# Joining the block inverses: which transposes VectorE runs first

## The chip, the cores and the metric

The kernel runs on one core of one Trainium2 chip. The metric is the device time of one execution in microseconds. The time before is the median of three runs, 4732.12 us (4730.72 to 4736.02).

## The reference, cut to what matters

The reference is a two-layer encoder trunk over two sequences of 1024 tokens (width 1024). Each layer projects its normalised input once, gives the columns to four mixers (A attention, B RWKV-7, C Mamba-2, D gated delta rule), gates their outputs and projects back. B and D run in both directions of time. D solves a unit triangular system in each chunk of 64 tokens:

```python
kb = k * beta[..., None]
m = jnp.where(strict, jnp.einsum('bhcld,bhcsd->bhcls', kb, k) * decay, 0.0)
tmat = m + jnp.eye(L, dtype=f32)
rhs = jnp.concatenate([v * beta[..., None], kb * jnp.exp(gc)[..., None]], axis=-1)
sol = lax.linalg.triangular_solve(tmat, rhs, left_side=True, lower=True)
```

B is a token-by-token scan in the reference (`S = S * w + (S a) b + v k`, output `S r`). The kernel computes it in chunks of 64 tokens too, with the same kind of triangular system.

## The kernel before, in words

**Inverses.** Each direction of B and of D needs the inverses of 64 unit triangular 64x64 matrices (4 heads, 16 chunks). The matrices lie as two halves `h` of 64 partitions with 32 matrices (`y`) each. `invert` (L529) gathers the two 32x32 diagonal blocks of each matrix with four VectorE transposes (L536) and inverts all blocks at once with 31 steps of two VectorE operations (L543, L544); the result is `r`, with 32 partitions for each of the four pairs of half and block. `merge` (L546), which this text calls the joining, makes the 64x64 inverses from them. Four transposes, one for each 32 partitions, put the inverted diagonal blocks back into `dst` (L551). Two more, one for each half, make the transposed copy `Tr` of one of the two blocks, shown in the profile as `mT` (L556). Then, for two groups `g` of 16 matrices: 32 first products on TensorE for each half (L565, off-diagonal block of the source times `Tr`) into a PSUM bank; a ScalarE copy for each half to `Qs`, shown as `mQ` (L567); 32 second products for each half (L571, `Qs` times the other diagonal block, read from `dst`); and a VectorE copy for each half of the result into the off-diagonal place of `dst` (L573). All products are 32x32x32. The PSUM pool has three banks (tag `b`), `mQ` and `mT` have one buffer each.

For D the source is `SC` and `dst` lies in `GT`, which the profile writes as `GT<-SC`; before the joining, GpSimd clears the opposite corner of `dst` (L1137) and VectorE writes the masked products beside it in `GT` (L1138, two operations). For B source and `dst` are the same tile `G`, and `r` is `iR`. What follows the joining is the chain over the 16 chunks (`gdn_chain`, `rwkv_chain`), whose first step reads the joined inverses.

**Units and sides.** There are four units, two sequences in each of two layers. In a unit the mixers form two serial strings that run beside each other: D then A on one side, C then B on the other (`mixers`, L590). Each unit has two joinings in D and two in B, so the program has 16.

**Background.** The projections into the mixers and out of them (`in_tile`, `out_tiles`) are L472 matmuls into `pj`. They belong to the next or the last unit and are laid beside the mixers (`ahead`, `behind`, `mix`, from L1646). `paced` (L470) binds them in groups of 5 or 8: the first matmul of a group releases a GpSimd memset of a token (L476), and the next group but one waits for it. Weights of the projections are split into two parts by ScalarE (L342) and VectorE (L343), and finished tiles are copied out by ScalarE (L325, L328) and VectorE (L326).

**Order of the work.** Nothing is ordered by hand within an engine. The program is written once, each instruction takes a priority from its place in the text, and a planner with a simulated timeline (`schedule_with_timeline_sim`, L1735) places the instructions of each engine in one fixed order when the kernel is built: of those that are ready in its timeline, the one with the first priority. Dependencies by the data are kept. `urgent()` (L484) moves a part ahead of all others; `invert`, `merge` and the chains after them are urgent, and so are the copies out of `pj` and the splitting of weights. All DMAs are issued from the SP queue (L145); the joining issues none.

Of the kernel before, what the change touches and what calls it, by code (L numbers as in the profile page):

```python
# [106 lines left out]
class Body:  # L107
# [438 lines left out]
    def merge(self, pool, psp, r, d, src, dst):  # L546

        nc = self.nc
        for q in range(4):
            h, j = q // 2, q % 2  # L550
            nc.vector.transpose(dst[h][32 * j:32 * j + 32, :, 32 * j:32 * j + 32].rearrange("p y t -> p t y"), r[32 * q:32 * q + 32].rearrange("p j t -> p t j"))  # L551
        a, b = (0, 32) if d == 0 else (32, 0)
        Tr = self.t(pool, [128, 32, 32], tag="mT")
        for h in range(2):
            A = slice(64 * h + a, 64 * h + a + 32)
            nc.vector.transpose(Tr[A].rearrange("p y j -> p j y"), r[A])  # L556
        for g in range(2):
            gs = slice(g * 16, g * 16 + 16)
            Qs = self.t(pool, [128, 16, 32], tag="mQ")
            p1 = [self.t(psp, [128, 512], tag="b") for _ in range(2)]  # L560
            at = [(64 * h + a, 64 * h + b) for h in range(2)]
            AB = [(slice(pa, pa + 32), slice(pb, pb + 32)) for pa, pb in at]
            for i in range(16):
                for h, (A, B) in enumerate(AB):
                    nc.tensor.matmul(p1[h][B, i * 32:i * 32 + 32], src[h][a:a + 32, g * 16 + i, b:b + 32], Tr[A, g * 16 + i, :], start=True, stop=True, tile_position=at[h])  # L565
            for h, (A, B) in enumerate(AB):
                nc.scalar.copy(Qs[B].rearrange("p i t -> p (i t)"), p1[h][B])  # L567
            p2 = [self.t(psp, [128, 512], tag="b") for _ in range(2)]
            for i in range(16):
                for h, (A, B) in enumerate(AB):  # L570
                    nc.tensor.matmul(p2[h][A, i * 32:i * 32 + 32], Qs[B, i, :], dst[h][b:b + 32, g * 16 + i, b:b + 32], start=True, stop=True, tile_position=at[h][::-1])  # L571
            for h, (A, B) in enumerate(AB):
                nc.vector.tensor_copy(dst[h][a:a + 32, gs, b:b + 32], p2[h][A].rearrange("p (i t) -> p i t", t=32))  # L573
# [1168 lines left out]
```

## Time and profile before

| | |
|---|---|
| median of 3 runs | 4732.12 us |
| profiled execution | 4724.56 us |
| its span | 4722.7 us |
| mean granted TensorE clock | 0.892 of full |
| busy: PE, weight load, VectorE, ScalarE, GpSimd | 89%, 67%, 64%, 38%, 8% |
| transposes of L551 | 64, 144.5 us |
| DMA traffic | 192 GB/s over the span |

The span is the stretch from the first to the last recorded instruction of the profiled execution, and the time of that execution holds 1.9 us around it. PE is TensorE, PEld its weight loads, which lie beside the matmuls. In rows in order of time, `x32` is a number of equal instructions merged into one row, and a bracket gives the idle time of the engine before the row and what ended it. The clock is that which the chip granted to TensorE, 1.0 being 2.4 GHz and 0.5 being 1.2 GHz.

### The profile page before, as it was taken

Reading aid. Unit: us, or ns where it says so; the run is one execution under the profiler, and the core shown is the slowest. Engines: PE = TensorE matmul, PEld = TensorE weight load, DVE = VectorE, ACT = ScalarE, POOL = GpSimd, SP = SyncE. Lnnn points to the kernel's source line nnn. Section 1 sums busy time; section 2 is a strip of 40 time slices with the busy share of each in tenths; the row PEclk is TensorE's granted clock in tenths of the full one; section 3 lists DMA queues with packets and bytes.
Section 4 is the critical chain, followed back from the end, with each engine's and each line's share of the span. In section 5 each row is a group of like instructions: output and inputs, shape, how many; then the busy total and the mean of one; then the engine's idle time right before and its main releaser. Section 6 shows DMA issues by size and latency. Waiting matters only on the chain. (4 is left out here: it accounts for less than half of the span.)

```text
span 4722.7 us, 98675 instructions
## 1 busy us (share of the span) xinstructions
PE 4204.5 (89%) x38484; PEld 3184.7 (67%) x38484; DVE 3013.8 (64%) x6237; ACT 1817.7 (38%) x4054; POOL 381.8 (8%) x2073
## 2 busy tenths in 40 slices
PE   6889988999998997989989898989897989979897
PEld 3667666667676776745757666867675766767676
DVE  2369487466479587477438858656743876865765
ACT  2432434462431434443434242435333324434433
POOL 0111001000011000000011100000001110000001
PEclk8899976998998987989989898889798999979898
DMA  5787764552676666564657665566355757665635
GB/s 211 283 257 250 244 180 147 182 151 72 196 233 209 201 206 191 176 194 148 225 193 243 243 220 159 182 189 189 106 179 180 233 202 228 205 210 159 175 112 171
DMA packets 518089, 912.85 MB, mean 193 GB/s; under 512 B 152312, under 2 KB 268536, under 8 KB 514040
## 3 DMA queue, kind: packets, MB, share of 16 engines
q1 hardware_dynamic: 517624, 906.54, 59.9%
q8 instruction: 305, 5.00, 0.4%
q14 instruction: 160, 1.31, 0.1%
HBM read 622.85 MB, written 283.43 MB: 192 GB/s over the span
## 5 line engine op out<-in xcount | busy, mean ns | idle before, releaser
L472 PE MATMUL pj<-hh,w 128*128 128x512 f32 (+1 forms) x4096 | 1431.1, 420 | 61.0 <-POOL token L476 27.6
L472 PEld LDWEIGHTS pj<-hh,w 128*128 128x128 f32 (+1 forms) x4096 | 785.0, 195 | 268.1 <-issue 40.8
L472 PE MATMUL pj<-hl,w 128*128 128x512 f32 (+1 forms) x2048 | 856.4, 418 | 16.5 <-POOL token L476 16.2
L472 PEld LDWEIGHTS pj<-hl,w 128*128 128x128 f32 (+1 forms) x2048 | 399.7, 195 | 116.3 <-POOL token L476 25.2
L476 POOL MEMSET token<- 1x1 f32 x1613 | 143.7, 89 | 3244.3 <-PE pj L472 3235.6
L472 PE MATMUL pj<-w,hh 128*128 128x256 f32 x1536 | 334.5, 308 | 9.3 <-POOL token L476 6.0
L472 PEld LDWEIGHTS pj<-w,hh 128*128 128x128 f32 x1536 | 261.6, 204 | 32.2 <-issue 9.4
L472 PE MATMUL pj<-w,hl 128*128 128x256 f32 x960 | 267.0, 305 | 0.2 <-DVE hl L377 0.2
L328 ACT COPY st<-pj 128x512 f32<-128x512 f32 (+1 forms) x192 | 111.6, 581 | 328.6 <-PE pj L472 285.9
L1575 ACT ACTIVATE pT<-b 128x512 f32<-128x512 f32 x256 | 149.8, 598 | 222.9 <-PE b L1573 218.8
L652 DVE SCALAR_TENSOR_TENSOR cva<-cvi,cw,cva 128x1024 f32<-128x1024 f32 x144 | 183.7, 1280 | 69.1 <-ACT cva L648 44.7
L1541 DVE TENSOR_REDUCE mx<-b 128x1 f32<-128x512 f32 x256 | 169.2, 685 | 63.9 <-PE b L1540 62.3
L342 ACT CAST w<-w 128x512 fp32r<-128x512 f32 x160 | 98.9, 620 | 247.6 <-DMA w<-w_in 173.8
L472 PEld LDWEIGHTS pj<-w,hl 128*128 128x128 f32 x960 | 185.2, 203 | 11.6 <-issue 3.6
L343 DVE TENSOR_TENSOR w<-w,w 128x512 fp32r<-128x512 f32 x160 | 113.5, 710 | 121.2 <-ACT w L342 118.2
L1219 ACT ACTIVATE SE<-SC,el 64x64 f32<-64x64 f32 x480 | 141.1, 338 | 117.9 <-DVE SC L1230 59.7
L938 DVE TENSOR_TENSOR ZS<-us,SE 64x128 f32<-64x128 f32 x240 | 69.1, 288 | 160.8 <-PE us L931 142.1
L843 DVE SCALAR_TENSOR_TENSOR G<-b,Dk,mk 128x128 f32<-128x128 f32 x512 | 142.1, 343 | 37.1 <-PE b L838 36.5
L838 PE MATMUL b<-AR,BK 64*64 64x128 f32 x2048 | 158.4, 318 | 5.3 <-DVE G L843 5.1
L1584 PEld LDWEIGHTS b<-VO,pT 128*64 128x64 f32 x4096 | 138.1, 143 | 31.8 <-issue 25.4
L1584 PE MATMUL b<-VO,pT 128*64 128x65 f32 x4096 | 153.8, 230 | 0.4 <-DVE mx L1541 0.3
L838 PEld LDWEIGHTS b<-AR,BK 64*64 64x64 f32 x2048 | 115.3, 155 | 46.7 <-issue 37.4
(395 smaller groups left out, 8179.1 us busy)
## 6 DMA issues: line engine op xcount, KB each, us to landing
w<-win SPq DMA_DIRECT2D x384, 512.0 KB
win<-w SPq DMA_DIRECT2D x128, 512.0 KB
P<-st SPq DMA_DIRECT2D x248, 256.0 KB
w<-wout SPq DMA_DIRECT2D x96, 512.0 KB
w<-w_in SPq DMA_DIRECT2D x128, 256.0 KB
G<-P SPq DMA_DIRECT2D x112, 256.5 KB
x<-x SPq DMA_DIRECT2D x56, 512.0 KB
cvi<-P SPq DMA_DIRECT2D x48, 512.0 KB
```

What stands on the lines that cost most here:

```text
L328: nc.scalar.copy(st[0:M], ps[0:M])
L342: nc.scalar.copy(w2[:, 0], w)
L343: nc.vector.tensor_tensor(w2[:, 1], w, wf[:, 0], SUB)
L472: m = self.nc.tensor.matmul(*mm[:3], **mm[3]).ins
L476: t = self.nc.gpsimd.memset(self.token, 0.0).ins
L652: nc.vector.scalar_tensor_tensor(a, c[:, j:j + 1024], wt(j, i), a, MUL, ADD)
L838: nc.tensor.matmul(pss[x][self.half(x ^ a), i * 128:i * 128 + 128], BK[self.half(x), pr, c, a], AR[self.half(x), pr, c].rearrange("p a t - ...
L843: v.scalar_tensor_tensor(G[:, x, pr, c, :], pss[x][:, i * 128:i * 128 + 128], Dk[:, c, 2 * x + pr:2 * x + pr + 1], mk, MUL, MUL)
L1219: nc.scalar.activation(SE[half(x), pr], VS[half(x), x, pr, i, :], AF.Identity, scale=el[half(x), d, pr, c:c + 1])
L1541: v.tensor_reduce(mx[:, n, qt:qt + 1], ps, AX.X, ALU.max, negate=True)
L1575: nc.scalar.activation(pT[kt], ps, AF.Exp)
L1584: nc.tensor.matmul(po[64 * x:64 * x + 64, i, :], pT[kt][:, o:o + 64], VO[:, kt, h, :], start=(kt == 0 and i == 0), stop=(kt == 7), skip_gr ...
```

## The change

In `merge` the loop of the four transposes into `dst` moves below the loop of the two transposes into `Tr`. Nothing else is changed.

```diff
     def merge(self, pool, psp, r, d, src, dst):
 
         nc = self.nc
-        for q in range(4):
-            h, j = q // 2, q % 2
-            nc.vector.transpose(dst[h][32 * j:32 * j + 32, :, 32 * j:32 * j + 32].rearrange("p y t -> p t y"), r[32 * q:32 * q + 32].rearrange("p j t -> p t j"))
         a, b = (0, 32) if d == 0 else (32, 0)
         Tr = self.t(pool, [128, 32, 32], tag="mT")
         for h in range(2):
             A = slice(64 * h + a, 64 * h + a + 32)
             nc.vector.transpose(Tr[A].rearrange("p y j -> p j y"), r[A])
+        for q in range(4):
+            h, j = q // 2, q % 2
+            nc.vector.transpose(dst[h][32 * j:32 * j + 32, :, 32 * j:32 * j + 32].rearrange("p y t -> p t y"), r[32 * q:32 * q + 32].rearrange("p j t -> p t j"))
         for g in range(2):
             gs = slice(g * 16, g * 16 + 16)
```

## Rows read from the trace of the kernel before

**Rows 1.** The page's busy shares and the 40 slices of PE.

```profile
PE 4204.5 (89%) x38484; PEld 3184.7 (67%) x38484; DVE 3013.8 (64%) x6237; ACT 1817.7 (38%) x4054; POOL 381.8 (8%) x2073
...
PE   6889988999998997989989898989897989979897
```

**Rows 2.** Waits of PE over the span: us in all, times, longest us.

```profile
PE b L565 <- DVE mT L556: 67.1, 21, 9.7
PE pj L472 <- POOL token L476: 50.1, 41, 4.9
```

**Rows 3.** The first joining in order of time: start us, us, engine, line, operation.

```profile
438.91 9.11 DVE L551 STREAM_TRANSPOSE GT<-SC 32x1024 f32<-32x1024 f32 x4
...
441.44 0.64 PE L472 MATMUL pj<-hh,w 128*128 128x512 f32 x2
...
446.72 0.39 PE L472 MATMUL pj<-hh,w 128*128 128x512 f32 x1
...
448.03 3.83 DVE L556 STREAM_TRANSPOSE mT<-SC 32x1024 f32<-32x1024 f32 x2
...
449.98 1.73 PE L565 MATMUL b<-mT,SC 32*32 32x32 f32 x32 [2.88 <-DVE mT L556]
451.74 0.58 ACT L567 COPY mQ<-b 32x512 f32<-32x512 f32 x1 [3.94 <-PE b L565]
...
454.29 4.58 DVE L1138 TENSOR_TENSOR GT<-EG,c_mi 64x2048 f32<-64x2048 f32 x2
...
456.19 2.52 PE L571 MATMUL b<-GT,mQ 32*32 32x32 f32 x61
...
462.19 1.05 PE L472 MATMUL pj<-hh,w 128*128 128x512 f32 x2
462.38 1.39 DVE L573 COPY GT<-b 32x512 f32<-32x512 f32 x2
```

**Rows 4.** Windows: first joining; then its transposes alone, and all 16 such stretches summed.

```profile
438.90:475.20 36.30, 31.01 (x326) 25.40 (x327) 32.78 (x27) 6.42 (x12) 3.40 (x18) 0.81 0.51 172
...
438.90:452.00 13.10, 7.81 (x59) 6.29 (x60) 12.98 (x7) 2.04 (x4) 2.42 (x8) 0.93 0.45 146
...
sum 208.60, PE 133.78 PEld 104.78 DVE 206.58 ACT 31.56 POOL 21.13; mean PE 8.36 PEld 6.55 DVE 12.91 ACT 1.97 POOL 1.32
```

**Rows 5.** Groups by line, whole span: busy us, mean ns; idle before, with releaser.

```profile
L551 DVE STREAM_TRANSPOSE GT<-SC 32x1024 f32<-32x1024 f32 x32 | 72.3, 2260 | 0.5
...
L571 PE MATMUL b<-GT,mQ 32*32 32x32 f32 x1024 | 49.3, 224 | 1.3 <-ACT mQ L567 1.3
...
L571 PE MATMUL b<-G,mQ 32*32 32x32 f32 x1024 | 44.3, 217 | 1.6 <-ACT mQ L567 1.6
```

**Rows 6.** Order of time, PE, last joining: first products without a wait.

```profile
4532.44 2.45 PE L565 MATMUL b<-mT,G 32*32 32x32 f32 x64
```

**Rows 7.** Order of time: the joining at 652, then six more long waits on PE.

```profile
652.15 9.02 DVE L551 STREAM_TRANSPOSE GT<-SC 32x1024 f32<-32x1024 f32 x4
...
658.28 0.39 PE L472 MATMUL pj<-hh,w 128*128 128x512 f32 x1
663.12 3.68 PE L565 MATMUL b<-mT,SC 32*32 32x32 f32 x61 [4.46 <-DVE mT L556]
...
1502.82 3.68 PE L565 MATMUL b<-mT,SC 32*32 32x32 f32 x61 [4.84 <-DVE mT L556]
...
1825.37 3.68 PE L565 MATMUL b<-mT,G 32*32 32x32 f32 x61 [9.68 <-DVE mT L556]
...
2684.33 3.68 PE L565 MATMUL b<-mT,SC 32*32 32x32 f32 x61 [5.11 <-DVE mT L556]
...
2883.41 3.85 PE L565 MATMUL b<-mT,SC 32*32 32x32 f32 x64 [5.13 <-DVE mT L556]
...
4020.46 1.82 PE L565 MATMUL b<-mT,SC 32*32 32x32 f32 x32 [4.15 <-DVE mT L556]
...
4175.84 1.91 PE L565 MATMUL b<-mT,G 32*32 32x32 f32 x32 [8.82 <-DVE mT L556]
```

## The prediction, made before the result was known

> **What bounds the kernel now.** I read the page's busy shares first [rows 1]: TensorE (PE) is busy for 89% of the span, VectorE (DVE) for 64%, and no slice of PE falls under six tenths. PE is the engine that is always loaded, because background projections (the `pj` matmuls of L472) are planned into every gap of the mixers' serial chains. So the time is PE's work plus PE's idle time: 4722.7 us of span less 4204.5 us busy leaves 518 us idle, and a change of order can win only there, or in the level of PE's clock.
>
> Then the waits of PE [rows 2]. The largest single row is the one that the change touches: the first products of the joining (L565) wait for the transposed copy `mT` of L556 for 67.1 us over 21 waits. The next row is 50.1 us (the pacing token).
>
> Then one joining in order of time [rows 3], the first of 16 (four units, two mixers, two directions). VectorE runs the four transposes of the diagonal blocks in 9.11 us and only then the two that make `mT`, 3.83 us. PE has background until 447.1 (446.72 + 0.39), idles 2.88 us, and starts the first products after the first `mT` transpose. Two copies on ScalarE follow; the second products (L571), which do read the diagonal blocks, start at 456.19, that is 4.33 us after the last transpose ended at 451.86. The reader is to see that the blocks transposed first are needed last.
>
> Last, the windows [rows 4]: the 16 stretches in which VectorE transposes are 208.6 us in sum, and PE is busy for 133.8 us of them. 74.8 us, or 4.7 us a joining, are idle; 67.1 of that is the wait of rows 2.
>
> **The change part by part.** It moves two instructions a joining ahead of four, on one engine; none is added or removed, and no DMA is issued by either. VectorE's own time stays: 4 x 2.26 [rows 5] + 3.83 [rows 3] = 12.87 us a joining, and nothing else on VectorE is passed.
>
> *First products earlier.* Both halves of `mT` are there 3.8 us after the transposes begin, instead of 12.9; the four others then run for 9.04 us beside PE. What can go beneath them: the 64 products of the first group, 2.45 us where PE did not wait [rows 6] and 3.85 us where it had idled [rows 7], and the copies of 0.58 us [rows 3]. That is at most 3.85 + 2 x 0.58 = 5.0 us, less than 9.04, so the cover suffices; were it gone (transposes shorter than 5 us), the rest would show again before the second products.
>
> *The wait added.* The second products now wait for the diagonal transposes, where before their row shows almost no wait (1.3 and 1.6 us on the copies [rows 5]). They can start 12.9 us after the transposes begin, against 17.3 in rows 3 (438.91 to 456.19). Queued behind them on PE stand the background matmuls, and behind these the copies of `pj` on ScalarE and the pacing token on POOL. The wait of all 16 together is bounded from below by nothing, if PE's planned background lasts, and from above by 16 x (9.04 - 2.45) = 105 us if the planner puts nothing between the products. The nearest row is the present wait, 67.1 us, since it comes from the same thing: the plan lets the transposes end sooner than they do. Rows 7 show it: in the joining at 652.15 PE's planned background ended at 658.67, 6.5 us after the transposes began, for a product that stands behind five of them; that is 1.3 us each, an estimate, where they take 2.2. So I take the idle time as unchanged, except where PE has nothing planned.
>
> *Where PE has nothing to do.* In seven joinings the wait is longer than the first products themselves: 4.46, 4.84, 9.68, 5.11, 5.13, 4.15 and 8.82 us [rows 7], 42.2 of the 67.1 us. There the 3.85 us of products drop into idle time and the chain behind them comes sooner by as much: 7 x 3.85 = 27 us. In the other nine (24.9 us of wait, 2.8 each) products and background only change places: gain between 0 and 24.9 us; I take 0, as background fills PE there.
>
> *The copies out (L573).* In rows 3 61 of the 64 second products of the first group are done at 458.71 and their copies start only at 462.38, since VectorE took 4.58 us of the mask product L1138 and other work first. With the second products nearer the transposes' end this may shrink or grow: from -3.7 us to +4.6 us for each of the eight joinings of the delta mixer, -30 to +37 us in all. I take 0, because PE went on with background in that time, and keep both ends.
>
> *Sum.* 4724.56 us (the profiled execution; its span is 4722.7) less 27 is 4697.6. The median of the runs shown is 4732.12, which is 7.6 us above the profiled execution; against it the forecast is 4705 us. A difference of 0.2%, about 9.5 us, is what can be told from no change here.
>
> **The rivals.**
>
> *All of the wait goes* (4665 us). If the first products give PE enough work to bridge all transposes, 67.1 us fall away. For it: 16 joinings each have 5 us that can be hidden. Against it: the second products take over a wait on the same 12.9 us.
>
> *The wait moves* (4732 us). The 67.1 us are then found before L571, PE does the same work with the same idle time, and a shorter chain only leaves more background for the ends of the units. For it: the estimate of 1.3 against 2.2 us a transpose holds in either order. Against it: the joinings of 8.8 and 9.7 us, where PE had nothing planned at all. The Trainium skill's Perfetto Trace Analysis, Identifying Performance Opportunities, says that kernels are generally made faster by improving the most-contended engine; by that rule an order on VectorE that takes nothing from PE's work gives 4732. Rows 1 agree on which engine it is, and rows 2 say that part of PE's time is a wait on the other one, so I give it a share and not the lead.
>
> *PE stops twice in a joining* (slower, 4750 us). Now one wait falls before the first products and one before the second, and the clock falls early. Rows 3 show its price: before the wait two `pj` matmuls take 0.64 us, at the level of 2.4 GHz (row at 441.44); 12 us after it, at 462.19, they still take 1.05 us, at 1.2 GHz. If the first products bring that level to the beginning of the stretch, the background beneath the transposes runs at it: some 26 matmuls in the stretch of the first joining (59 on PE [rows 4], less some 33 products), 13 x 0.41 = 5.3 us a joining, 85 us for 16. Idle time that remains (67.1 - 27 = 40 us) swallows part, the gain of 27 another: it decides from 67 / 5.3 = 13 joinings on, and at all 16 the net is +18. For it: the granted clock is 0.81 in the first whole joining and 0.93 in its transposes [rows 4], so the lower level comes with the small products. Against it: many stretches have little background. The Trainium skill's TensorE: Matmul & The Clock Gate, Part 1, has it that the throttled clock is the default and activity releases it; by that each added stop can bring the lower level back, and rows 3 agree for one stop.
>
> *The change does not do what it says.* In the RWKV mixer, products and diagonal blocks lie in one tile, `G`; were the planner to hold the products for writes to neighbouring columns, half of the gain would be gone (4719). Against it: the mask product L1138 writes columns of `GT` beside those of L551 and stands before it in the program, yet runs after it, at 454.29 [rows 3]; neighbouring columns do not bind.
>
> **How the numbers follow.** The first products hide in seven joinings: 0.45, own range 4688 to 4722. All of the wait goes: 0.13. The wait moves: 0.21. PE stops twice: 0.17. Half undone: 0.04. Any new order also moves the plan of the rest a little, which widens each case by some 10 us. Faster by more than 0.2% takes the first two nearly whole: 0.57; slower 0.18, the third rival and the tail of the second; the same 0.25. The range, 4655 to 4755 us, reaches to both outer cases and little past them.
>
> **What would show it.** The wait of L565 on `mT` should fall from 67.1 us to under 25 (the seven long ones to about 2 us each); L571 should get a row of waits on G and GT of L551. If that row stands near 67 us, the wait has moved; below 40, the step on the seven joinings is right. From the first transpose to the second products it should be about 13 us, not 17.3. If the granted clock over the transposes falls well below 0.9 while the time rises, the clock was the cause. The prediction is wrong if the wait of L565 falls and the span does not follow, or if the span falls by more than the PE waits do: then chains, not PE, set the end.

## The result, and the profile after

The changed kernel takes 4655.84 us (median of 4 runs, 4653.13 to 4670.07) against 4734.07 us (4730.72 to 4741.64) for the kernel before on the same chip: ratio 0.9838, 95% interval [0.9815, 0.9861]. That is 78 us faster. The forecast was 27 us, with a range of 4655 to 4755 us: the time lies just inside the range, at its fast end, and the gain is almost three times the one forecast. Beside two other sets of kernels it came out at 0.9829 [0.9795, 0.9863] and 0.9852 [0.9817, 0.9887].

The page after, answering [rows 1]: the span, the busy shares and the slices of PE. Lines of the changed kernel: the transposes into `mT` are L553, those of the diagonal blocks L556; all others kept their numbers.

```profile
span 4651.1 us, 98709 instructions
...
PE 4177.0 (90%) x38484; PEld 3160.9 (68%) x38484; DVE 3012.1 (65%) x6237; ACT 1818.2 (39%) x4054; POOL 385.0 (8%) x2073
...
PE   6888998999998987989988999889897999989997
```

VectorE does what it did (3012 us against 3014). PE is busy for 27.5 us less, though it runs the same 38484 instructions, and idle for 474.1 us against 518.2. These are single executions: two more traces of the changed kernel, from the series of `after_again` and `after_beside` below, have PE busy for 4195.0 and 4167.8 us and idle for 484.6 and 489.3.

The waits of PE after, answering [rows 2] (us in all, times, longest):

```profile
PE pj L472 <- POOL token L476: 59.2, 37, 4.9
...
PE b L571 <- DVE G L556: 12.5, 8, 3.0
PE b L565 <- DVE mT L553: 11.1, 9, 2.0
...
PE b L571 <- DVE GT L556: 4.7, 4, 2.2
```

The 67.1 us before the first products became 11.1, the longest of them 2.0 us where [rows 7] had up to 9.68, and the second products wait for 12.5 + 4.7 = 17.2 us. The three rows are 28.3 us together, 38.8 less than the one row before; the wait did not move.

The first joining in order of time, answering [rows 3]; DVE first, then PE:

```profile
443.36 3.89 DVE L553 STREAM_TRANSPOSE mT<-SC 32x1024 f32<-32x1024 f32 x2
447.28 8.96 DVE L556 STREAM_TRANSPOSE GT<-SC 32x1024 f32<-32x1024 f32 x4
...
445.31 1.19 PE L565 MATMUL b<-mT,SC 32*32 32x32 f32 x32 [1.98 <-DVE mT L553]
...
447.81 1.91 PE L565 MATMUL b<-mT,SC 32*32 32x32 f32 x32
...
454.22 1.31 PE L571 MATMUL b<-GT,mQ 32*32 32x32 f32 x32
...
456.83 1.10 PE L571 MATMUL b<-GT,mQ 32*32 32x32 f32 x29
```

Both blocks of first products end under the diagonal transposes. The second products start 10.9 us after the first transpose (454.22 less 443.36), while the fourth diagonal transpose still runs (to 456.24): one half's products need only that half's blocks. The forecast had 13 us, for all six transposes.

The products by line, answering [rows 5] (busy us, mean ns | idle before, with releaser):

```profile
L565 PE MATMUL b<-mT,SC 32*32 32x32 f32 x1024 | 45.6, 212 | 11.1 <-DVE mT L553 11.1
...
L571 PE MATMUL b<-G,mQ 32*32 32x32 f32 x1024 | 42.5, 210 | 13.4 <-DVE G L556 12.5 <-ACT st L386 0.9
...
L571 PE MATMUL b<-GT,mQ 32*32 32x32 f32 x1024 | 40.5, 202 | 4.8 <-DVE GT L556 4.7
L565 PE MATMUL b<-mT,G 32*32 32x32 f32 x1024 | 39.6, 213 | 0.0
```

The first products in the kernel before; its second products are in [rows 5]:

```profile
L565 PE MATMUL b<-mT,SC 32*32 32x32 f32 x1024 | 56.9, 228 | 34.6 <-DVE mT L556 32.4 <-ACT mQ L567 2.2
...
L565 PE MATMUL b<-mT,G 32*32 32x32 f32 x1024 | 48.5, 219 | 36.1 <-DVE mT L556 34.7 <-DVE G L573 1.3
```

The reader is to see the first number behind the bar, the busy time. The four groups are busy for 168.2 us; before they were busy for 56.9 + 49.3 + 48.5 + 44.3 = 199.0 us. The same products take 31 us less, and the prediction's sum had no term for it. The other two traces of the changed kernel give 169.2 and 162.5 us, and a kernel that keeps the old order (`swap_blocks` below) gives 193.8, so this fall is clear of what executions differ by. The fall of all of PE's busy time is not sized as well: by the three traces it lies between 9.5 and 36.7 us.

Windows after, answering [rows 4]: first joining, and its transposes alone (the last three columns are granted clock, DMA share, GB/s):

```profile
443.30:480.00 36.70, 33.43 (x356) 26.00 (x355) 36.12 (x36) 9.26 (x18) 4.11 (x22) 0.91 0.61 203
443.30:456.30 13.00, 11.02 (x116) 8.77 (x116) 12.81 (x8) 2.36 (x4) 2.33 (x7) 0.74 0.52 181
```

Over the transposes the clock fell from 0.93 to 0.74, as the rival of the two stops had it, but over the whole joining it rose from 0.81 to 0.91.

### The profile page after: what moved, and what is told of

It is laid out like the page before. It is cut to its first block, busy times and chain, and to the rows that moved or that the text cites. A ratio compares the mean times of both kernels' runs of the same rounds, so it can differ in the third digit from the quotient of the medians.

```text
span 4651.1 us, 98709 instructions
## 1 busy us (share of the span) xinstructions
PE 4177.0 (90%) x38484; PEld 3160.9 (68%) x38484; DVE 3012.1 (65%) x6237; ACT 1818.2 (39%) x4054; POOL 385.0 (8%) x2073
## 4 chain that ended last, share of the span: by engine, by line
PE 43%; DMA 15%; DVE 13%; ACT 3%; issue 3%; SPq 1%; POOL 1%; DVEq 0%; POOLq 0%; ACTq 0%
PE pj L472 20%; PE b L838 2%; PE b L1584 1%; DVE iA L536 1%; DVE G L556 1%; SPq L145 1%; DMA G<-P 1%; PE b L1540 1%; PE b L1571 1%; PE pj L244 1%; DMA UV<-vd 1%; PE b L571 1%; DMA st<-yd 1%; DVE iT L543 1%; DMA P<-st 1%
## 5 line engine op out<-in xcount | busy, mean ns | idle before, releaser
L938 DVE TENSOR_TENSOR ZS<-us,SE 64x128 f32<-64x128 f32 x240 | 69.1, 288 | 151.0 <-PE us L931 132.6
```

## The experiments

Every ratio is to the kernel before, on the same chip and in the same series; "us" is what the ratio leaves to 1, times the median of before in that series (4744 to 4750 us). The theory to test was that each joining gains by itself. The main rival was the new plan: the edit makes the planner place every matmul anew, and from the trace before to the one after the stretches from one joining to the next changed by anything from -30 to +22 us.

### Half of the joinings, and two exchanges

In `d_only` and `b_only` the new order holds in one mixer's joinings, under `if src is not dst:` and its opposite. In the two exchanges the old order stays; `swap_blocks` has the first of these edits, `swap_copy` the second:

```diff
-        for q in range(4):
+        for q in (2, 3, 0, 1):
...
-        for h in range(2):
+        for h in (1, 0):
```

> The new order in the eight joinings of the delta mixer alone (source and destination are different tiles); those of the RWKV mixer keep the old one. Theory 1 (each joining gains by itself: its first products hide under the four transposes, PE waits less and runs at the higher clock): about half of the whole gain of 78 us, so 4734 - 39 = 4695 us, with the wait of L565 gone in eight joinings and standing (some 30 us) in the other eight. Theory 2 (most of the gain is another plan, which came out better by chance): anywhere between 4656 and 4760, with no relation to the number of joinings changed.

> The new order in the eight joinings of the RWKV mixer alone. Theory 1: the other half of the gain, about 4695 us, and the two gains together 78 us within some 20. Theory 2: anywhere between 4656 and 4760, and the two gains do not add up to 78.

> The old order, with the four transposes of the diagonal blocks in the order of halves 1, 0 in place of 0, 1: the same work in front of the first products, so nothing to gain in a joining, but the planner starts from another text. Theory 1: 4734 us within 10. Theory 2, where a new plan alone moves the time by tens of us: more than 20 us away from 4734 to either side.

> The old order, with the two transposes into the copy mT in the order of halves 1, 0 in place of 0, 1. All six transposes still stand in front of most of the first products. Theory 1: 4734 us within 10. Theory 2: more than 20 us away from 4734 to either side; together with the other neutral order it gives the spread that a new plan alone brings.

Measured: `d_only` 0.9945 [0.9924, 0.9966], 26 us; `b_only` 0.9999 [0.9976, 1.0022], nothing, though the wait on `mT` in its joinings fell from 34.7 to 1.7 us, with 18.1 us new before the second products; `swap_blocks` 0.9994 [0.9976, 1.0013]; `swap_copy` 0.9955 [0.9929, 0.9981], 21 us, with 69.1 us of wait on `mT` as before. Halves of 26 and 0 don't make 78, and an exchange that should do nothing gave almost as much as one half. That spoke for the plan, and no edit that is planned anew could settle it.

### The plan held fixed

So the plan was taken out. The program is traced and planned in one form, the order of each engine is read off, and the program is built again in another form with every engine tied to that order; only the six transposes of a joining change places among themselves. Everything else stands as in the first plan, on all five engines. The traces of the kernel before and of `old_plan_new_order` bear this out: ScalarE, GpSimd and the DMA queue run the same instructions in the same order, VectorE differs in 64 places, all of them transposes of joinings, and on PE only records of near neighbours change places, as they do between two executions of one program. The old plan with the old order was not itself built in this way and timed.

```diff
+        for seq in () if plan is None else plan[1]:
+            for x, y in zip(seq, seq[1:]):
+                tc.add_manual_dep(tc.seen[y], tc.seen[x].name, NOSYNC, reason="plan")
```

> The changed kernel as it is, timed beside the three others on their chip. Both theories: ratio to the kernel before 0.982 to 0.987, some 70 us faster; PE's waits before the first products (L565) 11 us and before the second ones (L571) 17 us, as in its first trace. It gives the size that the two crossed kernels are to be measured against.

> The order of every engine is fixed to that which the planner made for the kernel before; only the six transposes of each joining run in the new order. Theory 1 (the wait itself was worth the time): L565's wait on mT falls from 67 us to under 15, at most 20 us come up before the second products, and the time falls by 40 to 60 us (ratio 0.987 to 0.992). Theory 2 (the new plan as a whole is worth the time): the wait goes too, but the time falls by less than 15 us (ratio above 0.997), since the rest of the plan is the old one.

> The order of every engine is fixed to that which the planner made for the changed kernel; only the six transposes of each joining run in the old order. Theory 1: the new plan puts the first products early, so they wait for all six transposes; L565's wait is 80 to 140 us and the time is that of the kernel before or more (ratio 0.995 to 1.01). Theory 2: the wait comes back but the time stays at 0.99 or below, since most of the gain sits in the plan of the rest.

| | old order of transposes | new order |
|---|---|---|
| old plan | 1 | 0.9863 [0.9828, 0.9898] |
| new plan | 1.0096 [1.0065, 1.0126] | 0.9829 [0.9795, 0.9863] |

The first theory holds. The order alone, with not one matmul moved, is worth 65 us; the new plan alone costs 46 us, and with the new order it adds some 16 us whose interval meets that of the order alone. With the new plan and the old order, PE waits twice as long as in the kernel before, since this plan calls for the first products earlier (L570 are the first products, L559 the transposes into `mT`):

```profile
PE b L570 <- DVE mT L559: 141.1, 25, 10.5
```

In the kernel with the old plan and the new order (lines from L565 on are five higher; L552 are its diagonal blocks), page and waits of PE:

```profile
PE 4172.1 (89%) x38484; PEld 3154.5 (67%) x38484; DVE 3016.1 (65%) x6237; ACT 1819.3 (39%) x4054; POOL 381.1 (8%) x2073
```

```profile
PE us L1216 <- DVE SC L1235: 23.3, 13, 8.0
...
PE b L576 <- DVE GT L552: 9.7, 5, 3.2
...
PE b L576 <- DVE G L552: 3.2, 2, 2.6
...
PE b L570 <- DVE mT L559: 1.0, 1, 1.0
```

Its products by line:

```profile
L570 PE MATMUL b<-mT,SC 32*32 32x32 f32 x1024 | 44.7, 207 | 2.2 <-ACT mQ L572 2.2
...
L576 PE MATMUL b<-GT,mQ 32*32 32x32 f32 x1024 | 43.1, 208 | 11.6 <-DVE GT L552 9.7 <-ACT mQ L572 1.3 <-DVE GT L578 0.5
...
L576 PE MATMUL b<-G,mQ 32*32 32x32 f32 x1024 | 41.6, 210 | 6.4 <-ACT mQ L572 3.2 <-DVE G L552 3.2
L570 PE MATMUL b<-mT,G 32*32 32x32 f32 x1024 | 41.0, 205 | 1.9 <-DVE mT L559 1.0 <-DVE G L578 0.8
```

Here the parts of the account can be read off, since the order of all else is equal. The waits of the joinings on their transposes fall from 67.1 to 13.9 us. The products' busy time falls from 199.0 to 170.4; the rest of PE's work takes 4001.7 us against 4005.5. The two falls are 81.8 us together, and PE's idle time only falls from 518.2 to 501.6 us (span 4673.7 less 4172.1), so waits elsewhere take back some 37 us by these traces; the chain's wait on `SC`, L1216 here, was 11.7 us in the kernel before. The size of that is not shown: the two traces are 49.0 us apart where the medians say 65, and the three traces of the changed kernel alone differ by 15 us of idle time and by 20 us in the rest of PE's work (4005.3 to 4025.8).

The joining at 652 of [rows 7] shows both gains at one place. First the kernel before, windows over its background and its first products; then the old plan with the new order, the same two windows and the rows of PE:

```profile
652.10:658.60 6.50, 5.38 (x20) 3.54 (x20) 6.44 (x4) 0.00 (x0) 2.33 (x7) 1.00 0.96 277
...
663.10:666.80 3.70, 3.65 (x68) 3.52 (x69) 3.67 (x2) 0.57 (x1) 0.00 (x0) 0.50 0.62 190
```

```profile
653.20:659.60 6.40, 5.28 (x20) 3.50 (x20) 6.30 (x4) 0.00 (x0) 2.33 (x7) 1.00 0.93 296
659.60:661.60 2.00, 2.00 (x67) 1.94 (x67) 2.00 (x1) 1.17 (x2) 0.00 (x0) 1.00 0.16 57
```

```profile
659.34 0.39 PE L472 MATMUL pj<-hh,w 128*128 128x512 f32 x1
659.66 2.04 PE L570 MATMUL b<-mT,SC 32*32 32x32 f32 x62
...
664.13 1.14 PE L576 MATMUL b<-GT,mQ 32*32 32x32 f32 x29 [1.42 <-DVE GT L552]
```

Behind the same background, without the idle 4.46 us, the first products run at 2.4 GHz (1.00) and take 2.04 us, where after the wait they ran at 1.2 GHz (0.50) and took 3.68 us for 61. A wait on PE is paid twice here: once as idle time and once in the matmuls behind it. The second payment depends on the plan. In the new plan with the old order the wait is 141.1 us, and yet the products take only 178.7 us, 10 to 16 more than in the three traces of the changed kernel; PE's idle time, 585.9 us there, is 97 to 112 more.

### Which joinings, under the fixed plan

> Engine orders fixed to the plan of the kernel before; the new order of the six transposes only in the eight joinings of the delta mixer (D). Planned anew, the same edit gave 24 us, and both mixers under the fixed plan gave 64 us. Theory 1 (each joining gains by itself, once the plan is fixed): 25 to 40 us faster, ratio 0.9915 to 0.9950. Rival (the plan decides, and B only looked worthless under its own new plan by chance or by nature): if B has nothing to give, D alone gives the whole, 50 to 65 us, ratio 0.986 to 0.9895.

> The same fixed plan; the new order only in the eight joinings of the RWKV mixer (B). Planned anew, this edit gave nothing (0.9999). Theory 1: 25 to 40 us faster (ratio 0.9915 to 0.9950), so that D and B add up to the 64 us of both, and the zero was the new plan's loss. Rival: within 10 us of the kernel before (ratio above 0.998), since background fills the wait of these joinings and the chain behind them has slack.

> Engine orders fixed to the plan of the kernel before; the new order of the six transposes only in the seven joinings whose wait was longer than the first products (4.46, 4.84, 9.68, 5.11, 5.13, 4.15 and 8.82 us, 42.2 us in all). The step of the prediction: these give 7 x 3.85 = 27 us, all that there is (ratio 0.9943). Theory 1 (each joining gives about its own wait and the slow products behind it): about 42 of the 67 us of wait, so some 40 of the 64 us, ratio 0.990 to 0.993. Third reading (the gain lies in the other nine): under 10 us, ratio above 0.998.

> The same fixed plan; the new order only in the other nine joinings (waits of 0 to 4.1 us, 24.9 us in all). The step of the prediction: nothing, products and background only change places (ratio 0.998 to 1.002). Theory 1: some 25 us, ratio 0.993 to 0.996, so that seven and nine add up to the 64 us of both. Third reading: 45 us or more, ratio below 0.991.

| new order in | old plan kept | planned anew |
|---|---|---|
| D only | 0.9916 [0.9897, 0.9935], 40 us | 0.9945, 26 us |
| B only | 0.9945 [0.9924, 0.9965], 26 us | 0.9999, 0 us |
| seven long waits | 0.9965 [0.9950, 0.9981], 17 us | |
| the other nine | 0.9937 [0.9919, 0.9956], 30 us | |

With the plan fixed the halves of D and B add up: 40 + 26 us against 65 for both, and the zero of B was its new plan's loss. A gain from building with tied orders as such would count twice in the two halves; by these figures it is 1 us, with the intervals of all three ratios on it. Divided as the prediction divided them, the seven give 17 us where 27 were forecast, and the nine give 30 where none was. The two sum to 47 us, less than 65, but the intervals of the three ratios leave room for that.

The first theory, that a joining gives its own wait and the slow products behind it, was off here in size: it had some 40 us for the seven, which hold 42.2 of the 67.1 us of wait. In their trace the wait on `mT` falls by 42.0 us, the second products wait for 11.0 us, and yet PE's idle time as a whole is 522.6 us against 518.2: the idle time came back outside these joinings. Where was not tried further.

### The clock by itself

In the old plan, with the old order and all transposes as late as ever, 14 matmuls that nobody reads stand before the first products of each joining, where PE idled (`p1` is overwritten by the products):

```diff
+                for _ in range(self.fill):
+                    nc.tensor.matmul(p1[0][:, 0:128], self.ident, self.blk, start=True, stop=True)
```

> The old plan and the old order of the transposes; only, 14 matmuls of the identity with a constant, which wait for nothing and are overwritten, stand on TensorE before the first products of each joining, so that some 3 us of its idle time there is filled with work. They take no time off the wait. Theory 1a (what is worth the time is the idle time itself): no gain, within 10 us of the kernel before or slower by up to 15. Theory 1b (part of the gain is the clock that TensorE loses in that idle time): the first products' median falls from 236 ns towards 191 ns and the time falls by 10 to 25 us although all transposes come as late as before.

0.9940 [0.9919, 0.9960]: PE has more work and no transpose comes sooner, and yet the kernel is 28 us faster, a little more than the 10 to 25 expected. Its groups (L567 the filler, two records for each matmul; L572 the first products):

```profile
L567 PE MATMUL b<-c_blk,c_ident 128*128 128x128 f32 x448 | 54.1, 279 | 0.0
...
L572 PE MATMUL b<-mT,SC 32*32 32x32 f32 x1024 | 48.4, 212 | 14.5 <-DVE mT L559 12.1 <-ACT mQ L574 2.2
...
L572 PE MATMUL b<-mT,G 32*32 32x32 f32 x1024 | 42.2, 206 | 13.3 <-DVE mT L559 12.6 <-DVE G L580 0.6
```

And the joining at 652 in it, on PE:

```profile
659.15 3.29 PE L567 MATMUL b<-c_blk,c_ident 128*128 128x128 f32 x28
663.86 1.19 PE L572 MATMUL b<-mT,SC 32*32 32x32 f32 x32 [1.42 <-DVE mT L559]
665.80 1.67 PE L572 MATMUL b<-mT,SC 32*32 32x32 f32 x29 [0.74 <-DVE mT L559]
```

The first block of 32 records now takes 1.19 us, half of the 2.45 us that 64 take at full clock [rows 6], though it waits for the same transposes. All products fall from 199.0 to 179.1 us. PE's other work, filler apart, falls from 4005.5 to 3989.2 us, which is within what executions of one kernel differ by. The mean granted clock is 0.901 over the 12 runs (0.895 to 0.908) against 0.889 over the 21 of before beside them (0.883 to 0.894). So the reading that idle time alone counts is wrong: a good part of what the order gives can be had from the clock alone. How the 65 us split between the two can't be read from this, as the filler also holds the clock up in places that the new order leaves alone.

### Better orders, and how far plans lie apart

> The changed kernel, in which the two diagonal blocks that the second products read are transposed directly behind the copies, and the two that no product reads come last. It is planned anew. Theory 1: L565's wait stays near 11 us and L571's falls from 17 to under 8 us; 5 to 12 us faster than the changed kernel. Theory 2: the same waits, but the time is anywhere within 25 us of the changed kernel, as another plan comes out.

> Engine orders fixed to the plan of the changed kernel; behind the two copies come first the two diagonal blocks that the second products read, then the other two. Planned anew this order gave only 31 us (0.9930). Theory 1: the wait of the second products (17 to 21 us) falls below 6 us and the time is 0 to 20 us below that of the changed kernel (ratio 0.978 to 0.983), so the loss was the plan's. Rival: the order itself is the worse one (the two late blocks delay something else) and the ratio stays at 0.990 or above.

> The changed kernel with its four diagonal blocks in the order 2, 3, 0, 1, planned anew: the half that waits first is the other one, so the work that can be hidden is the same. It is to show how far plans of the same worth lie apart. Theory 1: waits on mT and on the diagonal blocks together 20 to 40 us, and any ratio between 0.978 and 0.996, since the new plan adds some 20 to 30 us of its own to either side. Rival (a plan moves the time by 10 us at most): ratio 0.981 to 0.985.

```diff
-        for q in range(4):
+        for q in (b // 32, 2 + b // 32, a // 32, 2 + a // 32):
```

The needed blocks first, planned anew: 0.9930 [0.9908, 0.9952]. The same order on the plan of the changed kernel: 0.9796 [0.9773, 0.9820], the best ratio of all, 97 us. The first lost nothing in its joinings (waits 9.9 us on `mT`, 5.9 us on the blocks); its plan runs the rest of PE's work in 4052.9 us, against 4005.3 to 4025.8 in the three traces of the changed kernel. `new_blocks`, the same work as the changed kernel with the halves exchanged, came to 0.9892 [0.9872, 0.9912], with 38.7 us of wait on the blocks instead of 17.2; with the 10.6 on `mT` that is more than was expected, so it is not a plan of the same worth. So one order in two plans lay 14 us (D), 26 us (B) and 64 us (needed blocks first) apart.

Last, the 21 us of `swap_copy`. By its row below, the planner had put the products of the two halves in turn, where the plan before has one half's block behind the other's. All its products are busy for 157.9 us (199.0 before), while PE's idle time is 552.6 us (518.2). Its joining at 669, first products, and the window over them:

```profile
669.12 1.92 PE L565 MATMUL b<-mT,SC 32*32 32x32 f32 x64 [6.24 <-DVE mT L556]
```

```profile
669.10:671.10 2.00, 1.92 (x64) 1.78 (x64) 2.00 (x1) 0.03 (x1) 0.00 (x0) 0.50 0.89 299
```

At 1.2 GHz the 64 take 1.92 us; in [rows 7] 61 take 3.68 us at the same clock. `alternate` puts them in turn by hand, in the plan of the changed kernel with the needed blocks first (L569 are the first products, L578 the copies out):

```diff
+    for m in tc.pairs:
+        both = list(range(m, m + 32))
...
+        s[:] = head + both + [n for n in s[k:] if not m <= n < m + 32]
```

> The plan of the changed kernel, the needed diagonal blocks first (0.9796), and besides, the products of the two halves stand in turn (half 0, half 1, half 0, ...) where the plan has them as one block behind the other; the block that stood first moves back to the place of the second. Reading A (products of the two halves overlap on TensorE, as 64 in 1.92 us at granted clock 0.50 in the kernel with the copies exchanged say, against 3.68 us one block behind the other): busy time of L565 and L571 falls from 157 us to under 110 us, and the time by another 20 to 45 us (ratio 0.970 to 0.976). Reading B (the busy time falls, but the time does not follow, since the first half's copies and second products come later): ratio 0.979 to 0.988.

> The changed kernel with its two copies in the order half 1, half 0, planned anew. In the old order this exchange made the plan put the products of the halves in turn and gave 21 us (0.9955) with the waits unchanged. If products in turn are the cause, busy time of L565 and L571 falls below 140 us again and the ratio is 0.975 to 0.983; if the 21 us were the luck of that plan, the busy time stays near 168 us or the ratio comes out at 0.984 or above.

> The changed kernel once more, on the chip of the two others, so that they can be told from it: ratio 0.981 to 0.986 by all readings.

```profile
PE b L569 <- DVE GT L578: 60.5, 8, 12.1
...
PE b L569 <- DVE G L578: 11.2, 5, 3.9
```

```profile
447.05 1.20 PE L569 MATMUL b<-mT,SC 32*32 32x32 f32 x64
...
466.61 1.91 PE L569 MATMUL b<-mT,SC 32*32 32x32 f32 x62 [12.07 <-DVE GT L578]
```

`alternate` came to 0.9876 [0.9845, 0.9907], 59 us, worse than the 97 us without the turns. Its products are busy for only 102.1 us (157.0 before), but the pool has three banks, and both halves of the second group now need a bank at once, so they wait for the copies out of the first group (L578): 71.7 us, against 2.4 without the turns. The time is that of reading B; the wait that came up is on the banks, which the reading did not name. `new_copy`, planned anew, came to 0.9923 [0.9897, 0.9948] with the products at 152.2 us: their busy time fell (from 168.2), and the kernel is slower than the changed one. By what was expected of it, the 21 us of `swap_copy` were its plan's luck; what in that plan gave them stays open. The changed kernel beside them: 0.9852. `new_plan_needed_first` ran in another series; its interval meets those of the changed kernel at their edge, so that it is the faster one is likely and not shown.

## Why the prediction was wrong

*What bounds the kernel now* held. PE sets the time; the two engines that the edit touches do the same work, and the span fell by 27.5 us of PE's busy time and 44.1 of its idle time. The sign that the prediction named against itself came up, the span falling by more than the PE waits (71.6 us against 38.8), and the reason given there, that chains and not PE set the end, is not what the traces show: most of the rest, 27.5 of 32.8 us, is PE's own busy time, and under the fixed plan idle time outside the joinings grew instead of falling.

*First products earlier* held: in the first joining both blocks of products and their copies lie under the diagonal transposes.

*The wait added* is the step that failed, at "So I take the idle time as unchanged, except where PE has nothing planned." It had the wait stay as long in a new place; the idle time fell by 44.1 us, not by 27. The estimate that it stands on was usable: the 1.3 us for a transpose come from one joining, and by the same reckoning 13 of the 16 give 1.2 to 2.0, where it takes 2.2. Its conclusion was not. By that estimate the error adds up over the transposes ahead of a product, and the runs agree: with five or six of them the wait was 67.1 / 16 = 4.2 us a joining, with one or two it is 11.1 / 16 = 0.7 us. That the planner's durations are the reason is argued; no run changes them. The second products stand behind up to six again, but behind the first products and copies as well; they wait for 17.2 us in all, not for "the present wait, 67.1". Why the plan is late enough there was not tried further.

*Where PE has nothing to do* failed with it. Under the fixed plan the nine joinings costed at 0 give 30 us and the seven costed at 27 give 17. The test named for it (a row of waits at L571 below 40 us shows it right) was no test: the row was 17.2 us, and the nine had gained as well.

*A term was missing*: the clock behind the wait. The prediction had both prices in hand, 2.45 us in [rows 6] and 3.85 in [rows 7] for the 64 first products, and used the larger only to ask whether the cover suffices. Taking these 1.4 us off in each of the 15 joinings that waited would have added 21 us. Under the fixed plan the first products lost 19.7 us of busy time and the second ones 8.9, 28.6 together.

*The copies out (L573)*, costed at 0, was not taken apart. In the first joining the second products of the first group are done at about 458 and their copies start at 466.16, some 8 us later, against 3.7 before: nearly the loss that the prediction had as its worst case, in a joining where PE went on with background.

Of the rivals, *all of the wait goes* came nearest (4665 us), for part of the reason: 53 of 67 us of wait went under the fixed plan and 39 in the changed kernel, and the products' busy time fell beside it. That the sum of such parts came so near is in part luck, as the new plan shares in it. *The wait moves* fell. *PE stops twice* saw the clock fall over the transposes of the first joining, but over the whole of it the clock rose; the two stops together are 28.3 us in all joinings, where the one that they replaced was 67.1. Its argument that "the lower level comes with the small products" did not hold: at 652, behind background without a stop, they run at 1.00. The width given for "the plan of the rest", some 10 us, was too small: one order in two plans lay 14 to 64 us apart.

## What to carry to other kernels

A wait on a loaded TensorE costs its idle time and then the slower clock of the matmuls behind it, so add both from the trace; the second part can be large (29 us beside 53 of wait in the old plan) or small (10 to 16 beside 113 in the new). Where a planner orders the work, an edit's own effect and its new plan's are of one size: hold the plan fixed to tell them apart, and carry the edit over to the better plan. The wait here grew with the number of transposes ahead of the waiting products, in either plan (1.0 against 67.1 us, 11.1 against 141.1), so put the ones they need first.

## What the runs showed of the hardware beside that

Small products of the two halves, which stand at different positions of the array, overlap when they stand in turn: 64 records in 1.20 us at 2.4 GHz and 1.92 us at 1.2 GHz, where one position's block behind the other's takes 2.45 us [rows 6] and some 3.7 us. Work that fills idle time on TensorE and whose result nobody reads made the kernel 0.6% faster. Two executions of the changed kernel had spans of 4651.1 and 4679.6 us at mean clocks of 0.895 and 0.893, and their stretches from one joining to the next differ by up to 11 us, so single traces can't tell joinings apart by such stretches, and whole runs were compared instead.
